# The second layer's modulation: from K-tile matmuls to sums on VectorE

## The chip, the cores and the metric

The kernel runs on one core of one Trainium2 chip. TensorE does matmuls, VectorE and ScalarE elementwise work, GpSimd little here; SyncE (SP) issues nearly all DMAs. All engines run side by side and each works through its own queue in order. The metric is device microseconds of one execution; lower is better.

## The reference, cut to what matters

Two layers over 256 latent tokens and 256 context tokens of width 1024. Each layer begins with a modulation that depends on nothing but the two condition vectors:

```
ada_lat = silu(c) @ w_ada[layer] + b_ada[layer]          # 1024 -> 6144
ada_ctx = silu(c_ctx) @ w_ada[layer] + b_ada[layer]
sh1, sc1, g1, sh2, sc2, g2 = split(ada_lat, 6)           # the same six for ctx
u = modulate(rmsnorm(h, gains[0]), sh1, sc1)             # x * (1 + sc) + sh
h = h + g1 * rmsnorm(mixer(u), gains[1])
h = h + g2 * rmsnorm(mlp(modulate(rmsnorm(h, gains[2]), sh2, sc2)), gains[3])
```

In the second (last) layer the context goes into the mixer only (`need_ctx` is false): of the context's six parts only `sh1` and `sc1` are used there. The MLP is `square(relu(x @ w1)) @ w2`, 1024 to 4096 to 1024.

## The kernel before

Both streams lie side by side as 512 columns of activations. Every big product is computed in split precision: a weight tile of 128x2048 is loaded into one of two `raw` buffers (`ra` in the traces, `RAW=2`), ScalarE rounds each half of it to `wh` (128x1024), VectorE writes the rest `wl = ra - wh`, and TensorE makes three matmuls per K-tile: with `wh` and the rounded activations, `wh` and their rest, `wl` and the rounded ones (`weight`, line 552). `wh` and `wl` have four buffers each (`WB=4`), so a half can be ready while TensorE works on up to three others.

The order of the program is that of a scheduler that models the engines; what is written under a high priority comes first. Background work comes in generators in a queue `bg`: each call of `bg.step()` runs the first generator to its next `yield`. In layer 0, after the output projection, `bg` gets the second layer's modulation in three parts s = 0, 1, 2 of 2048 columns each and the second layer's filters (lines 1492 to 1495). The steps are then taken once for each of the 16 weight tiles of the first MLP product (line 1546) and of those of the second (line 1558, 8 tiles for each half of the output columns), and what is left is drained where layer 1 begins (line 1561).

`ada_steps` (line 366) takes, for each of eight K-tiles, a `raw` buffer, loads 128x2048 of `w_ada` into it and multiplies it with `cst[:, k, :]`: 128 x 32 with silu(c) and silu(c_ctx) in columns 0 and 1 and zeros elsewhere. The four matmuls of a K-tile write four strips of 32 partitions of one PSUM tile and run side by side; a matmul in f32 shows as two instructions in the trace, so a K-tile is a group of eight, `px<-ra,k`. After eight K-tiles the PSUM tile is copied, transposed and put into columns (`ada_cols`, used by `modulation`), and for s > 0 multiplied with gains and written to DRAM as gate rows.

`AM` (line 315) are four 128x512 tiles for the masked scores of the HGRN2 branch. Their upper triangles must be zero, since `copy_predicated` (line 975) writes the others only. They are idle between the branch of layer 0 and that of layer 1.

In the second MLP product `hpart` (line 1498) splits the activations on VectorE as well: a `CAST` to the rounded part and a subtraction for the rest, four K-tiles for each weight tile, shared by the four token tiles.

Of the kernel before, what the change touches and what calls it, by code (L numbers as in the profile page):

```python
# [148 lines left out]
def body(tc, I, out, cfg=None):  # L149
    ctx = ExitStack()  # L150
    with ctx:
        _body(ctx, tc, I, out, cfg or CFG)
# [7 lines left out]
def _body(ctx, tc, I, out, cfg):  # L160
# [12 lines left out]
    def nm(s):  # L173
        counter[0] += 1
        return f"{s}{counter[0]}"

    def blk(dt=F32, p=128, w=512, late=""):

        x = bp.tile([p, w], dt, tag="b", name=nm("b"), padded_shape=[128, 512])
        if late and late in cfg["LATE"]:  # L180
            nc.gpsimd.memset(x[:, 0:1].bitcast(F32) if dt is not F32 else x[:, 0:1], 0.0)
        return x

    def tmp(dt=F32, p=128, w=512, late=""):
        x = tp.tile([p, w], dt, tag="t", name=nm("t"), padded_shape=[128, 512])
        if late and late in cfg["LATE"]:
            nc.gpsimd.memset(x[:, 0:1], 0.0)
        return x
# [4 lines left out]
    def psm():  # L193
        return pm.tile([128, 512], F32, tag="m", name=nm("pm"))

    def psx(kind):
        for i, (kinds, n) in enumerate(cfg["PX"]):
            if kind in kinds:
                return px.tile([128, 512], F32, tag=f"x{i}", name=nm("px"), bufs=n)

    def kt(shape, dt=F32, name="k"):
        return keep.tile(shape, dt, name=nm(name))
# [22 lines left out]
    dve, act, pe, pool = InOrder(nc.vector), InOrder(nc.scalar), InOrder(nc.tensor), nc.gpsimd  # L225
# [20 lines left out]
    def sigmoid():  # L246
        era("sigmoid_and_others")
# [7 lines left out]
    def tt(o, a, b, op):  # L255
        dve.tensor_tensor(o, a, b, op=op)

    def mul(o, a, b):
        tt(o, a, b, ALU.mult)

    def add(o, a, b):
        tt(o, a, b, ALU.add)
# [4 lines left out]
    def stt(o, a, s, b, op0=ALU.mult, op1=ALU.add):  # L267
        dve.scalar_tensor_tensor(o, a, s, b, op0=op0, op1=op1)

    def ts(o, a, s1, s2=None, op0=ALU.mult, op1=ALU.add):  # L270
        if s2 is None:
            dve.tensor_scalar(o, a, s1, None, op0=op0)
        else:
            dve.tensor_scalar(o, a, s1, s2, op0=op0, op1=op1)

    def mm(p, l, r, start, stop, **k):
        return pe.matmul(p, l, r, start=start, stop=stop, **k).ins
# [8 lines left out]
    dma = nc.sync.dma_start  # L286
# [18 lines left out]
    def col(l, name, i, n=1):  # L305
        return vec[l][:, V[name] + i:V[name] + i + n]
# [7 lines left out]
    AM = []  # L314
    for d in range(4):
        a_t = kt([128, 512])
# [3 lines left out]

    cst = kt([128, 8, 32])
    pool.memset(cst, 0.0)
    csg = kt([128, 8, 2])
    sigmoid()
    fn(csg, cc, AF.Sigmoid)
# [4 lines left out]
    def raw_tile():  # L330
        return wp.tile([128, 2048], F32, tag="raw", name=nm("ra"), bufs=cfg["RAW"])
# [34 lines left out]
    def ada_steps(l, s):  # L366
        acc = psx('a')
        for k in range(8):
            raw = raw_tile()
            dma(raw, I["w_ada"][l, k * 128:k * 128 + 128, s * 2048:s * 2048 + 2048])  # L370
            with tc.high_priority(cfg["AP"]):
                for j in range(4):
                    mm(acc[32 * j:32 * j + 32, :], cst[:, k, :], raw[:, j * 512:j * 512 + 512], k == 0, k == 7,
                       tile_position=(0, 32 * j))
            yield
        rows = tmp()
        dve.tensor_copy(rows, acc)
        pt = psx('a')
        for b in range(4):
            pe.transpose(pt[:, b * 128:b * 128 + 128], rows[:, b * 128:b * 128 + 128], ident)  # L380
        cols = kt([128, 2, 2, 8], name="ac")
        pv = pt.rearrange("p (b j r) -> p r j b", b=4, j=4)
        for r in range(2):
            add(cols[:, r].rearrange("p m (j b) -> p (m j) b", b=4), pv[:, r],
                col(l, "ba", 16 * s, 16).rearrange("p (m b) -> p m b", b=4))
        ada_cols[l, s] = cols
        if s > 0:
            w, j0 = s - 1, 2 * (s - 1)
            gr, br = tmp(), tmp()
            dma(gr, I["gate_rows"][l, w, :, 0])  # L390
            dma(br, I["gate_rows"][l, w, :, 1])
            add(rows, rows, br)
            mul(gr, gr, rows)
            st = dr.tile([2, 2, 512], F32, name=nm("gd"))
            for n in range(2):
                dma(st[:, n, :], gr[32 * (j0 + n):32 * (j0 + n) + 2, :])
            G_rows[l, w] = st
        yield

    def modulation(l, which):  # L400
# [320 lines left out]
    def groups(g, sizes):  # L721

        for n in sizes:
            for _ in range(n):
                next(g)
            yield
        for _ in g:
            yield
# [448 lines left out]
    bg = Pump()  # L1177


    def layer(l, S, xs=None, es=None):  # L1180
# [9 lines left out]
        if l == 1:  # L1190
            raw, bd = raw_tile(), [[None, None], [None, None]]
            for d in range(2):
                for g in range(2):
                    r = raw[:, (2 * d + g) * 512:(2 * d + g) * 512 + 512]
# [128 lines left out]
        pv = [psm() for _ in range(4)]  # L1323
        for r in range(2):
            ws = wide(I["w_i"][l, r])
            for t in range(4):
                for kk in range(4):
                    k = 4 * r + kk
# [69 lines left out]
        m = [blk(late='m' if l == 1 else '') for _ in range(8 // per)]  # L1398
        M = None
        gone = False  # L1400
        for bi, b in enumerate(cfg["ORD"][l]):
# [10 lines left out]
            for r in range(2):  # L1412
# [3 lines left out]
                for i in range(4 * r // per, 4 * (r + 1) // per):  # L1416
                    p = psm()
                    for j in range(per):
                        c = i * per + j - 4 * r
# [5 lines left out]
                    x, a, b_ = m[i], m[i], gates[i]  # L1425
                    if bi == 2 and l == 1:
                        x = tmp()
                        a, b_ = (y.rearrange("p (j c r) -> p j c r", j=2, r=ROWS) for y in (a, b_))
# [61 lines left out]


        if full:
            for s in range(3):
                bg.put(ada_steps(1, s))
            bg.put(groups(filters(1), cfg["FG"]))
        hb, cache = [], {}

# [14 lines left out]
        else:  # L1512
            for r in range(2):
                pt = psx('n')
# [9 lines left out]
        for r in range(0 if full else 2, 16):  # L1524
# [12 lines left out]
            for p in ps:  # L1537
                a, x = tmp(), blk() if full else tmp()
# [183 lines left out]
    for _ in f0:  # L1722
        pass
    bg.put(ada_steps(0, 1))
    bg.put(ada_steps(0, 2))
    S1, es = layer(0, S0, xs)
    layer(1, S1, None, es)


# [14 lines left out]
```

## Time and profile before

| | us |
|---|---|
| median of 3 runs | 1521.4 (1518.2 to 1522.33) |
| the profiled execution | 1519.12 |
| its span, first to last instruction | 1517.3 |
| TensorE busy in it | 1487.6 |
| VectorE busy | 953.8 |
| ScalarE busy | 747.6 |

The profile shows one execution. A group of its table is all instructions with the same engine, operation, tiles and shape; `L217` is the helper through which they are recorded, so the tile names tell them apart. `b`, `t` and `pm`/`px` are pools of blocks, temporaries and PSUM tiles, `k` is any tile that is kept (so `cst`, the identity and the score buffers all read `k`), `h` the residual stream. A timeline row has the start, the length from the first start to the last end, and the count of merged instructions; matmuls overlap, so the starts tell more than the lengths.

### The profile page before, as it was taken

To read this page: it belongs to the slowest core of one execution; us is meant where nothing else is said; L and a number is where in the kernel's file an instruction comes from. 1 tells how busy PE (TensorE), PEld (TensorE's weight loads), DVE (VectorE), ACT (ScalarE), POOL (GpSimd) and SP (SyncE) were. 2 spreads that over 40 slices of the span, in tenths; PEclk is the share of its full clock that TensorE was granted. 3 is DMA by queue.
4 is the path that set the end of the run, shared out by engine and by line. 5 is a ranking of instruction groups with operands and counts; after the bars stand their busy time and mean duration, and the time that the engine had idled before them with its cause. 6 is when DMAs were issued, how large, how long until landed. Compare 5 with 4: busy or idle time off the path is not lost.

```text
span 1517.3 us, 21665 instructions
## 1 busy us (share of the span) xinstructions
PE 1487.6 (98%) x8534; PEld 1228.1 (81%) x8534; DVE 953.8 (63%) x1651; ACT 747.6 (49%) x1188; POOL 20.8 (1%) x234
## 2 busy tenths in 40 slices
PE   7999999999999999999999999999999999999998
PEld 4766877788888888777777777798889999899986
DVE  5776396987535277212135657676989986866544
ACT  6476555543232426433331122567887655565433
POOL 0000000000000000000000000000000000000000
PEclk8999999999999999999999999999999999999999
DMA  9644334323222241543554553322233435444553
GB/s 299 238 186 154 122 139 154 125 72 124 84 89 106 88 162 57 222 166 139 195 203 157 181 183 108 115 98 100 108 112 130 163 140 198 178 157 177 209 194 111
DMA packets 47270, 225.38 MB, mean 149 GB/s; under 512 B 4912, under 2 KB 14768, under 8 KB 23488
## 3 DMA queue, kind: packets, MB, share of 16 engines
q1 hardware_dynamic: 45440, 220.85, 41.0%
q10 hardware_dynamic: 1728, 3.15, 0.6%
q8 instruction: 67, 1.10, 0.3%
q14 instruction: 35, 0.29, 0.1%
HBM read 220.80 MB, written 3.18 MB: 148 GB/s over the span
## 4 chain that ended last, share of the span: by engine, by line
PE 82%; DVE 9%; ACT 4%; DMA 3%; issue 1%; SPq 0%; DVEq 0%; ACTq 0%; POOL 0%; POOLq 0%
PE pm L217 71%; PE px L217 10%; DVE b L217 4%; DVE t L217 3%; ACT b L217 2%; DVE wl L217 2%; DMA ra<-in_w_ada_dram 2%; ACT t L217 1%; ACT wh L217 1%; DMA b<-in_w_ada_dram 1%; DMA ra<-in_w_in_dram 1%; DMA h<-in_x_dram 1%; ACT L217 1%; DVE s L217 0%; DVE h L217 0%
## 5 line engine op out<-in xcount | busy, mean ns | idle before, releaser
L217 PE MATMUL pm<-b,wh 128*128 128x512 f32 (+1 forms) x3264 | 823.7, 342 | 1.7 <-DVE b L217 1.7
L217 PEld LDWEIGHTS pm<-b,wh 128*128 128x128 f32 x3264 | 563.9, 190 | 79.9 <-issue 9.3
L217 DVE TENSOR_TENSOR wl<-ra,wh 128x1024 fp32r<-128x1024 f32 x278 | 338.8, 1223 | 380.8 <-ACT wh L217 372.3
L217 PE MATMUL pm<-b,wl 128*128 128x512 f32 (+1 forms) x1632 | 558.0, 342 | 0.9 <-DVE wl L217 0.9
L217 ACT ACTIVATE wh<-ra 128x1024 fp32r<-128x1024 f32 x278 | 293.0, 1059 | 512.3 <-PE pm L217 471.3
L217 PEld LDWEIGHTS pm<-b,wl 128*128 128x128 f32 x1632 | 309.8, 190 | 43.8 <-issue 9.7
L217 PE MATMUL pm<-wh,b 128*128 128x512 f32 x976 | 304.1, 392 | 0.0
L217 PEld LDWEIGHTS pm<-wh,b 128*128 128x128 f32 x976 | 182.2, 188 | 46.8 <-issue 7.4
L217 PE MATMUL pm<-wl,b 128*128 128x512 f32 x488 | 191.2, 392 | 0.0
L217 DVE TENSOR_TENSOR b<-b,b 128x512 fp32r<-128x512 f32 (+2 forms) x179 | 120.8, 682 | 49.4 <-PE pm L217 32.9
L217 PEld LDWEIGHTS pm<-wl,b 128*128 128x128 f32 x488 | 91.6, 188 | 22.4 <-issue 3.6
L217 PE MATMUL pm<-b,b 128*128 128x256 f32 (+1 forms) x456 | 77.5, 324 | 2.3 <-DVE b L217 2.2
L217 ACT ACTIVATE t<-t 128x512 f32<-128x512 f32 (+3 forms) x124 | 61.0, 525 | 32.6 <-DVE t L217 31.7
L217 PEld LDWEIGHTS pm<-b,b 128*128 128x128 f32 x456 | 66.7, 190 | 11.0 <-DVE b L217 3.6
L217 ACT ACTIVATE t<-pm 128x512 f32<-128x512 f32 (+1 forms) x74 | 42.5, 576 | 62.6 <-PE pm L217 60.1
L217 ACT ACTIVATE b<-pm 128x512 f32<-128x512 f32 x88 | 50.8, 584 | 22.9 <-PE pm L217 13.0
L217 PE MATMUL px<-b,b 128*128 128x128 f32 (+1 forms) x280 | 55.5, 344 | 2.1 <-ACT b L217 1.3
L217 ACT ACTIVATE b<-b 128x512 f32<-128x512 f32 (+1 forms) x80 | 48.9, 628 | 10.8 <-DVE b L217 9.6
L217 ACT ACTIVATE b<-b,k 128x512 f32<-128x512 f32 x64 | 45.9, 739 | 8.5 <-DVE b L217 8.3
L217 PEld LDWEIGHTS px<-b,b 128*128 128x128 f32 x280 | 38.7, 190 | 12.6 <-issue 5.6
L217 PE MATMUL px<-ra,k 128*32 128x512 f32 x320 | 42.0, 604 | 2.4 <-DMA ra<-in_w_ada_dram 2.1
L217 DVE TENSOR_TENSOR t<-t,b 128x512 f32<-128x512 f32 (+2 forms) x78 | 42.0, 563 | 0.1
(107 smaller groups left out, 1018.1 us busy)
## 6 DMA issues: line engine op xcount, KB each, us to landing
ra<-in_w_mlp_dram SPq DMA_DIRECT2D x63, 1024.0 KB, 4.8
ra<-in_w_in_dram SPq DMA_DIRECT2D x58, 1024.0 KB, 4.8
ra<-in_w_ada_dram SPq DMA_DIRECT2D x40, 1024.0 KB, 4.9
ra<-in_w_proj_dram SPq DMA_DIRECT2D x12, 1024.0 KB, 4.8
b<-in_w_ada_dram SPq DMA_DIRECT2D x32, 256.0 KB, 6.0
ra<-in_w_out_dram SPq DMA_DIRECT2D x8, 1024.0 KB, 4.8
ra<-in_w_i_dram SPq DMA_DIRECT2D x4, 1024.0 KB, 5.0
b<-gd SPq DMA_DIRECT2D x12, 256.0 KB, 5.5
```

Of the source, the lines that this page charges most:

```text
L217: r = f(*a, **k)
```

## The change

`ada_steps` keeps the first layer's parts. The second layer's come from a new generator, `ada_second`. It loads `w_ada` in pieces of 128x512 into the four score buffers, in 24 steps of four pieces. VectorE multiplies each piece with the condition's value of each partition (a column of `cst`) and adds it to a running sum of 128x512 in a temporary. For s = 0 two sums are kept for each piece (latent and context) and the steps run over eight K-tiles of the first 1024 columns and then of the second; for s = 1 and 2 there is the latent's sum alone. A piece's buffer is loaded for the next step as soon as its sums are issued. When eight K-tiles are added up, four matmuls with `sel` (ones in one column of 32) add the 128 partitions and put the result where the old groups put theirs; for s = 0 that happens twice, once for each half of the columns, into two rows of the same PSUM tile. What follows is `ada_out`, cut out of `ada_steps`, with a second layout for s = 0. At the end GpSimd zeroes the score buffers.

```
@@ -320,6 +320,10 @@
 
     cst = kt([128, 8, 32])
     pool.memset(cst, 0.0)
+    sel = kt([128, 2, 32])
+    pool.memset(sel, 0.0)
+    for r in range(2):
+        pool.memset(sel[:, r, r:r + 1], 1.0)
     csg = kt([128, 8, 2])
     sigmoid()
     fn(csg, cc, AF.Sigmoid)
@@ -373,16 +377,25 @@
                     mm(acc[32 * j:32 * j + 32, :], cst[:, k, :], raw[:, j * 512:j * 512 + 512], k == 0, k == 7,
                        tile_position=(0, 32 * j))
             yield
+        ada_out(l, s, acc, "(j r)")
+        yield
+
+    def ada_out(l, s, acc, order):
+
         rows = tmp()
         dve.tensor_copy(rows, acc)
         pt = psx('a')
         for b in range(4):
             pe.transpose(pt[:, b * 128:b * 128 + 128], rows[:, b * 128:b * 128 + 128], ident)
         cols = kt([128, 2, 2, 8], name="ac")
-        pv = pt.rearrange("p (b j r) -> p r j b", b=4, j=4)
+        if order == "(j r)":
+            pv = pt.rearrange("p (b m n r) -> p r m n b", b=4, m=2, n=2)
+        else:
+            pv = pt.rearrange("p (b n r m) -> p r m n b", b=4, n=2, r=2)[:, :, :2]
         for r in range(2):
-            add(cols[:, r].rearrange("p m (j b) -> p (m j) b", b=4), pv[:, r],
-                col(l, "ba", 16 * s, 16).rearrange("p (m b) -> p m b", b=4))
+            for m in range(2):
+                add(cols[:, r, m].rearrange("p (n b) -> p n b", b=4), pv[:, r, m],
+                    col(l, "ba", 16 * s + 8 * m, 8).rearrange("p (n b) -> p n b", b=4))
         ada_cols[l, s] = cols
         if s > 0:
             w, j0 = s - 1, 2 * (s - 1)
@@ -395,6 +408,58 @@
             for n in range(2):
                 dma(st[:, n, :], gr[32 * (j0 + n):32 * (j0 + n) + 2, :])
             G_rows[l, w] = st
+
+    def ada_second():
+
+
+        plans = [(s, i) for s in range(3) for i in range(8)]
+
+        def pieces(s, i):
+
+            if s > 0:
+                return [(i, s * 2048 + n * 512, n) for n in range(4)]
+            half, kk = divmod(i, 4)
+            return [(2 * kk + a, half * 1024 + n * 512, n) for a in range(2) for n in range(2)]
+
+        def load(q, plan):
+            k, c, _ = pieces(*plan)[q]
+            dma(AM[q], I["w_ada"][1, k * 128:k * 128 + 128, c:c + 512])
+
+        for q in range(4):
+            load(q, plans[0])
+        acc = None
+        for at_, (s, i) in enumerate(plans):
+            yield
+            rs = (0, 1) if s == 0 else (0,)
+            if i == 0 or (s == 0 and i == 4):
+                sums = {}
+            for q, (k, _, n) in enumerate(pieces(s, i)):
+                for r in rs:
+                    c = cst[:, k, r:r + 1]
+                    if (r, n) in sums:
+                        stt(sums[r, n], AM[q], c, sums[r, n])
+                    else:
+                        sums[r, n] = tmp()
+                        ts(sums[r, n], AM[q], c)
+                if at_ + 1 < len(plans):
+                    load(q, plans[at_ + 1])
+            if s == 0 and i in (3, 7):
+                if i == 3:
+                    acc = psx('a')
+                with tc.high_priority(cfg["AP"]):
+                    for g in (3, 0, 1, 2):
+                        mm(acc[32 * g:32 * g + 32, :], sel[:, i // 4, :], sums[g % 2, g // 2], i == 3, i == 7,
+                           tile_position=(0, 32 * g))
+                if i == 7:
+                    ada_out(1, s, acc, "(n r m)")
+            elif i == 7:
+                acc = psx('a')
+                with tc.high_priority(cfg["AP"]):
+                    for g in (3, 0, 1, 2):
+                        mm(acc[32 * g:32 * g + 32, :], sel[:, 0, :], sums[0, g], True, True, tile_position=(0, 32 * g))
+                ada_out(1, s, acc, "(j r)")
+        for a_t in AM:
+            pool.memset(a_t, 0.0)
         yield
 
     def modulation(l, which):
@@ -1490,8 +1555,7 @@
 
 
         if full:
-            for s in range(3):
-                bg.put(ada_steps(1, s))
+            bg.put(ada_second())
             bg.put(groups(filters(1), cfg["FG"]))
         hb, cache = [], {}
```

How this moves the instructions is shown at three places. `wh1012`/`wl1013` and so on are weight halves; numbers differ between the kernels, names of pools don't.

First place, the first of the new groups, in the first MLP product. TensorE before: a group of the fifth to eighth K-tile amid a half's 24 matmuls (`k17` is `cst`, `px980` the accumulator).

```order
L217 MATMUL pm1017_5475<-b833_4546,wh1014_5470 128x512
L217 MATMUL pm1017_5475<-b825_4538,wl1015_5471 128x512
L217 MATMUL pm1017_5475<-b826_4539,wh1014_5470 128x512
L217 MATMUL pm1017_5475<-b834_4547,wh1014_5470 128x512
L217 MATMUL px980_5295<-ra1046_5680,k17_103 32x512 x4
L217 MATMUL pm1017_5475<-b826_4539,wl1015_5471 128x512
L217 MATMUL pm1017_5475<-b827_4540,wh1014_5470 128x512
L217 MATMUL pm1017_5475<-b835_4548,wh1014_5470 128x512
```

After, the first group: `t985` to `t988` are the four sums of the first 1024 columns, `k18` is `sel`. It stands behind 14 of a half's 24 matmuls.

```order
L217 MATMUL pm1016_5501<-b828_4548,wl1013_5494 128x512
L217 MATMUL pm1016_5501<-b829_4549,wh1012_5493 128x512
L217 MATMUL pm1016_5501<-b837_4557,wh1012_5493 128x512
L217 MATMUL px1022_5571<-t988_5322,k18_105 32x512
L217 MATMUL px1022_5571<-t985_5315,k18_105 32x512
L217 MATMUL px1022_5571<-t986_5317,k18_105 32x512
L217 MATMUL px1022_5571<-t987_5320,k18_105 32x512
L217 MATMUL pm1016_5501<-b829_4549,wl1013_5494 128x512
L217 MATMUL pm1016_5501<-b830_4550,wh1012_5493 128x512
```

Four matmuls on a `raw` tile have become four on four sums; this kernel has four such groups, 24 before.

VectorE in front of that group: the last seven sums (`k13` to `k16` are the score buffers, `k17` is `cst`) and two `wl`. Before, only `wl` of one weight tile after another stand here.

```order
L217 TENSOR_TENSOR wl1025_5579<-ra1023_5576,wh1024_5578 128x1024
L217 SCALAR_TENSOR_TENSOR t986_5317<-k13_95,k17_103,t986_5317 128x512
L217 SCALAR_TENSOR_TENSOR t987_5320<-k14_97,k17_103,t987_5320 128x512
L217 SCALAR_TENSOR_TENSOR t988_5322<-k14_97,k17_103,t988_5322 128x512
L217 SCALAR_TENSOR_TENSOR t985_5315<-k15_99,k17_103,t985_5315 128x512
L217 SCALAR_TENSOR_TENSOR t986_5317<-k15_99,k17_103,t986_5317 128x512
L217 SCALAR_TENSOR_TENSOR t987_5320<-k16_101,k17_103,t987_5320 128x512
L217 TENSOR_TENSOR wl1027_5583<-ra1023_5576,wh1026_5582 128x1024
L217 SCALAR_TENSOR_TENSOR t988_5322<-k16_101,k17_103,t988_5322 128x512
L217 TENSOR_TENSOR wl1040_5663<-ra1038_5660,wh1039_5662 128x1024
```

The group waits for the sum `t988`, which stands behind the `wl` of a weight half that is two halves further on than the one in which the group stands.

Second place, VectorE in the second MLP product, from the `wl` of one weight tile to those of the next. Before (`b1237<-b1081` and the row behind it are a split):

```order
L217 TENSOR_TENSOR wl1230_6706<-ra1228_6703,wh1229_6705 128x1024
L217 TENSOR_TENSOR b1234_6714<-b1067_5821,b1233_6713 128x512
L217 TENSOR_TENSOR wl1232_6710<-ra1228_6703,wh1231_6709 128x1024
L217 CAST b1235_6720<-b1069_5825 128x512
L217 TENSOR_TENSOR b1236_6721<-b1069_5825,b1235_6720 128x512
L217 CAST b1237_6727<-b1081_5899 128x512
L217 TENSOR_TENSOR b1238_6728<-b1081_5899,b1237_6727 128x512
L217 CAST b1239_6734<-b1083_5903 128x512
L217 TENSOR_TENSOR b1240_6735<-b1083_5903,b1239_6734 128x512
L217 TENSOR_TENSOR wl1244_6786<-ra1242_6783,wh1243_6785 128x1024
```

After:

```order
L217 TENSOR_TENSOR b1232_6833<-b1068_5881,b1231_6832 128x512
L217 CAST b1233_6839<-b1070_5885 128x512
L217 SCALAR_TENSOR_TENSOR t1196_6646<-k13_95,k17_103,t1196_6646 128x512
L217 TENSOR_TENSOR b1234_6840<-b1070_5885,b1233_6839 128x512
L217 CAST b1235_6846<-b1082_5977 128x512
L217 SCALAR_TENSOR_TENSOR t1197_6649<-k14_97,k17_103,t1197_6649 128x512
L217 SCALAR_TENSOR_TENSOR t1198_6652<-k15_99,k17_103,t1198_6652 128x512
L217 SCALAR_TENSOR_TENSOR t1199_6655<-k16_101,k17_103,t1199_6655 128x512
L217 TENSOR_TENSOR b1236_6847<-b1082_5977,b1235_6846 128x512
L217 CAST b1237_6853<-b1084_5981 128x512
L217 SCALAR_TENSOR_TENSOR t1196_6646<-k13_95,k17_103,t1196_6646 128x512
L217 TENSOR_TENSOR b1238_6854<-b1084_5981,b1237_6853 128x512
```

Sums stand between the two rows of a split; from one weight tile's `wl` to the next there are four splits as before, and six sums.

Third place, SP in the first MLP product. Before, loads of weights and of `w_ada` alternate:

```order
L549 DMA ra1023_5538<-in_w_mlp1_dram 128x2048
L370 DMA ra1034_5606<-in_w_ada_dram 128x2048
L549 DMA ra1035_5612<-in_w_mlp1_dram 128x2048
L370 DMA ra1046_5680<-in_w_ada_dram 128x2048
L549 DMA ra1047_5686<-in_w_mlp1_dram 128x2048
L370 DMA ra1058_5754<-in_w_ada_dram 128x2048
```

After, weight tiles follow the ring of `raw` alone, and the pieces stand between them:

```order
L426 DMA k13_95<-in_w_ada_dram 128x512
L614 DMA ra1038_5660<-in_w_mlp1_dram 128x2048
L426 DMA k14_97<-in_w_ada_dram 128x512
L426 DMA k15_99<-in_w_ada_dram 128x512
L426 DMA k16_101<-in_w_ada_dram 128x512
L426 DMA k13_95<-in_w_ada_dram 128x512
L426 DMA k14_97<-in_w_ada_dram 128x512
L426 DMA k15_99<-in_w_ada_dram 128x512
L614 DMA ra1049_5740<-in_w_mlp1_dram 128x2048
L426 DMA k16_101<-in_w_ada_dram 128x512
```

A piece waits in SP's queue for the sums that read its buffer, and a weight tile for the `wl` that reads its own; each holds back what stands behind it.

## Rows read from the trace of the kernel before

**Rows 1.** The page: busy us of each engine, share, instructions.
```profile
PE 1487.6 (98%) x8534; PEld 1228.1 (81%) x8534; DVE 953.8 (63%) x1651; ACT 747.6 (49%) x1188; POOL 20.8 (1%) x234
```

**Rows 2.** Stretches of 40 us: busy us (instructions), granted clock, DMA share, GB/s.
```profile
core 0: us, PE busy (x) PEld busy (x) DVE busy (x) ACT busy (x) POOL busy (x), PEclk, DMA share, GB/s
680.00:720.00 40.00, 40.00 (x189) 30.41 (x187) 9.50 (x14) 15.29 (x21) 0.00 (x0) 1.00 0.36 131
840.00:880.00 40.00, 39.92 (x185) 30.09 (x184) 24.35 (x39) 7.51 (x8) 0.00 (x0) 1.00 0.51 182
```

**Rows 3.** Waits of TensorE, 560 to 1000 us: total, times, longest.
```profile
PE px L217 <- DMA ra<-in_w_ada_dram: 0.9, 1, 0.9
```

**Rows 4.** Timeline of TensorE around one group: start, length, instructions.
```profile
665.65 0.62 PE L217 MATMUL pm<-b,wh 128*128 128x512 f32 x2
...
666.33 0.61 PE L217 MATMUL pm<-b,wh 128*128 128x512 f32 x2
...
666.87 1.06 PE L217 MATMUL px<-ra,k 128*32 128x512 f32 x8
...
667.87 0.50 PE L217 MATMUL pm<-b,wl 128*128 128x512 f32 x1
...
668.21 0.62 PE L217 MATMUL pm<-b,wh 128*128 128x512 f32 x2
```

**Rows 5.** Timeline of TensorE: starts of six groups of the second layer.
```profile
607.31 1.92 PE L217 MATMUL px<-ra,k 128*32 128x512 f32 x16
...
750.80 1.07 PE L217 MATMUL px<-ra,k 128*32 128x512 f32 x8
...
762.90 1.07 PE L217 MATMUL px<-ra,k 128*32 128x512 f32 x8
...
812.62 1.06 PE L217 MATMUL px<-ra,k 128*32 128x512 f32 x8
...
819.85 1.06 PE L217 MATMUL px<-ra,k 128*32 128x512 f32 x8 [0.91 <-DMA ra<-in_w_ada_dram]
...
884.37 1.06 PE L217 MATMUL px<-ra,k 128*32 128x512 f32 x8
```

**Rows 6.** Groups of instructions: count, busy us, mean ns, idle before and releasers.
```profile
L217 DVE TENSOR_TENSOR wl<-ra,wh 128x1024 fp32r<-128x1024 f32 x278 | 338.8, 1223 | 380.8 <-ACT wh L217 372.3 <-PE pm L217 3.6 <-PE px L217 2.3
...
L217 ACT ACTIVATE wh<-ra 128x1024 fp32r<-128x1024 f32 x278 | 293.0, 1059 | 512.3 <-PE pm L217 471.3 <-DVE b L217 26.8 <-DMA ra<-in_w_in_dram 7.5
...
L217 DVE TENSOR_TENSOR b<-b,b 128x512 fp32r<-128x512 f32 (+2 forms) x179 | 120.8, 682 | 49.4 <-PE pm L217 32.9 <-ACT b L217 12.9 <-DVE b L217 0.5
...
L217 DVE CAST b<-b 128x512 fp32r<-128x512 f32 x89 | 37.5, 421 | 3.8 <-ACT b L217 2.4 <-PE pm L217 1.0
...
L217 DVE SCALAR_TENSOR_TENSOR h<-t,s,h 128x512 f32<-128x512 f32 x24 | 17.0, 748 | 0.4
...
L217 DVE TENSOR_SCALAR t<-h,s,s 128x512 f32<-128x512 f32 x28 | 14.0, 544 | 0.8
```

**Rows 7.** Timeline of VectorE, first and second MLP product: idle before, releaser.
```profile
749.94 1.23 DVE L217 TENSOR_TENSOR wl<-ra,wh 128x1024 fp32r<-128x1024 f32 x1 [4.21 <-ACT wh L217]
...
850.52 0.69 DVE L217 TENSOR_TENSOR b<-b,b 128x512 fp32r<-128x512 f32 x1 [6.44 <-PE pm L217]
```

**Rows 8.** DMA issues: count, KB each, median us from issue to landing.
```profile
ra<-in_w_ada_dram SPq DMA_DIRECT2D x40, 1024.0 KB, 4.9
...
t<-in_gate_rows_dram SPq DMA_DIRECT2D x8, 256.0 KB, 5.3
...
ra<-in_bd_dram SPq DMA_DIRECT2D x4, 256.0 KB, 2.7
...
t<-in_decay_dram SPq DMA_DIRECT2D x2, 256.0 KB, 6.8
```

**Rows 9.** Timeline of SP between two groups: issues of a weight and a `w_ada` tile.
```profile
751.92 0.33 SPq L549 DMA_DIRECT2D ra<-in_w_mlp_dram  x1
757.88 0.33 SPq L370 DMA_DIRECT2D ra<-in_w_ada_dram  x1
```

## The prediction

> **What bounds the kernel now.** I read four views in this order. First the busy line of the page: TensorE is at work 1487.6 of 1517.3 us, VectorE 953.8 [rows 1]. Then the stretches in which the changed work lies: from 680 to 720 us and from 840 to 880 us TensorE is busy for all, or all but 0.1, of the 40 us, at the full granted clock (1.00, the 2.4 GHz level), while VectorE works 9.5 and 24.4 of 40 us [rows 2]. Third, who made TensorE wait between 560 and 1000 us: one row, 0.9 us in all, for a load of `w_ada` [rows 3]. Fourth, TensorE's timeline, because a busy engine need not be a useful one. The reader is to see there that big matmuls follow each other every 0.227 us (three in 0.68 us, 665.65 to 666.33), that a modulation group starts at 666.87 and that the next big matmul starts at 667.87 [rows 4].
>
> The Trainium skill says in "Perfetto Trace Analysis", section "Identifying the Most-Contended Engine", that matmul busy time is a poor measure for TensorE and that LDWEIGHTS busy is a better one. By it the 81% of weight loads [rows 1] leave room, groups could sit in bubbles, and the change would be worth nothing; that is the third rival below. The trace speaks against it by starts instead of busy time, in the next paragraph.
>
> **What is removed.** The second layer's modulation runs as 24 groups of eight TensorE instructions (four matmuls in two passes), the first two at 607.31, the last at 884.37. Two neighbours are 12.10 us apart (750.80 to 762.90) with 48 big matmuls between [rows 5]. These take 48 x 0.227 = 10.88 us. So a group costs 1.22 us of TensorE's time, its 1.06 us plus refilling the array, and it fills no bubble. 24 x 1.22 = 29.3 us. The one wait for a load, 0.9 us [rows 3, 5], goes as well: 30.2 us. The `wh` and `wl` of the weights stay.
>
> **What is added on TensorE.** Four groups of the same eight instructions (two for s = 0, one each for s = 1 and 2), with a sum in place of the raw tile. Their form is that of the removed ones, so 4 x 1.22 = 4.9 us. Transposes and the copies behind them stay in number. If nothing else happened the balance would be -25.3 us.
>
> **What is added on VectorE.** 64 multiplications and sums for s = 0 (32 pieces, two rows each), 32 each for s = 1 and 2: 128 instructions, of which 16 begin a sum (`tensor_scalar`) and 112 add to one. The nearest rows are of the same shape and memory: `h<-t,s,h` 17.0 us for 24, so 0.71 us of the engine each (0.75 from start to end), and `t<-h,s,s` 14.0 for 28, 0.50 us [rows 6]. 16 x 0.50 + 112 x 0.71 = 88 us. It lies beside TensorE's work, in idle time of 30 of 40 us in the first MLP product and 16 of 40 in the second [rows 2]. The cover is real as long as VectorE's own products for TensorE come in time, and the engine works in order, so I follow what is queued behind a sum.
>
> In the first MLP product these are the weight halves `wl`. They run up to three halves (16 us) ahead of TensorE: VectorE waits for `wh`, and that for TensorE to release a buffer [rows 6, 7]. Six or seven sums between two `wl` make 1.22 + 6.5 x 0.71 = 5.8 us for a half on which TensorE works 24 x 0.227 = 5.44 us. That is 0.4 us of backlog for each of about four halves, and the 16 us swallow it: nothing.
>
> In the second MLP product VectorE also splits four tiles of activations for each weight tile. From the release of a weight buffer it needs 1.06 (`wh`) + 2 x 1.22 (`wl`) + 4 x (0.42 + 0.675) for the splits [rows 6] + 6 x 0.71 for the sums queued among them = 12.1 us. TensorE wants the last split after its 48 matmuls and nine more, 57 x 0.227 = 12.9 us. Before, without the sums and with a group in the step, VectorE had 6.44 us to spare here [rows 7]; now 0.8 us. I take 2 us for five such steps; the bounds are 0 and 8 (a load late by some 1.6 us in each).
>
> **The new waits.** TensorE now waits for a sum where it waited for a load, and the four groups stand in its queue close behind the moment at which the sum can be ready. Group 1 stands 14 matmuls (3.2 us) behind the end of the half that frees a weight buffer, and its last sum is queued behind that buffer's `wl`: 1.06 + 1.22 + 0.75 = 3.0 us, and hand-overs. A hand-over is short: a group begun at 750.80 ends at 751.87 and the load that waits for it is issued at 751.92 [rows 5, 9]; I allow 0.2 us for three. With some backlog, 0.5 us of waiting. Group 2: 26 matmuls, 5.9 us, against 1.06 + 1.22 + 5 x 0.71 + 0.2 = 6.0: 0.5 with backlog. Group 3: 23 matmuls, 5.2 us, against 1.06 + 1.22 + 4 x 0.71 + 0.2 = 5.3: 0.4 with a late load. Group 4: 44 matmuls, 10.0 us, against 1.06 + 2.44 + 5 x 0.42 + 4 x 0.675 + 5 x 0.71 + 0.2 = 12.0: 1.8 to 2.0, I take 1.8. Together 3.2 us. Behind a waiting group stand all big matmuls, so each of these microseconds is lost in full; behind a waiting sum stand `wl` and the splits, priced above.
>
> **The loads.** The same bytes of `w_ada` come as 96 pieces of 256 KB instead of 24 of 1 MB. No row shows such a piece into a score buffer. The nearest: the four `bd` pieces of 256 KB land 2.7 us after issue, a gate row piece 5.3, a decay piece 6.8 [rows 8]. With 2.7 a score buffer goes round in 0.75 + 0.05 + 0.33 (issue, [rows 9]) + 2.7 = 3.8 us. For s = 1 the order leaves 5.4 us for a K-tile (its eight K-tiles stand beside eight halves of 5.44 us), for s = 2 about 7.6 (5.75 sums to a step of 10.9 us, four sums to a K-tile), for s = 0 about 6.9 (eight sums and one `wl`). I take the `bd` row, the one of the same kind (several pieces back to back, from an otherwise quiet queue), so nothing is late; the 5.3 and 6.8 rows carry two rivals. Weight loads get the whole two-tile ring again: a `w_ada` tile was issued at 757.88, a ring's turn behind a weight tile at 751.92 [rows 9]. That helps them start earlier and frees no time on TensorE, which did not wait for them.
>
> The Trainium skill says in "DMA: Bandwidth & Descriptors", section "Queues, rings and completion order", that the loads of one issuing engine share its rings and are taken in order. By it a piece issued right behind a 1 MB weight tile cannot land before it. The row that bears on it agrees: a 1 MB tile lands after 4.9 us, and the gate row issued behind one after 5.3 [rows 8]. If that held for every second K-tile, half of the next case's delay would come, and the sum would be -16, or 1506 us.
>
> **Other parts.** The two memsets of `sel` and four of the score buffers lie on GpSimd, which is 1% busy [rows 1]. The first four pieces are loaded during layer 0. The filters of the second layer now come earlier, under TensorE's full stretch instead of at the layers' junction; TensorE waits at neither [rows 3]. I count all three as nothing, with 2 us to either side for layer 0's shifted order.
>
> **Sum.** -30.2 + 4.9 + 3.2 + 2.0 = -20.1 us. Against the profiled execution (1519.1 us; its span is 1517.3) that is 1499.0. The median of the runs is 1521.4, 2.3 above it, so 1501.3 on that footing: I say 1501.
>
> **Rivals.** *Late pieces, still faster.* If the pieces land like the gate row (5.3 us), a buffer's turn is 6.4 us, 1.0 more than the order leaves for s = 1: seven refills make 7 us at group 3. For s = 0, where two sums use a piece, the turn is 7.2 against 6.9: 2 us over both halves. 9 us of waiting more: -11, 1510 us. For it: pieces stand behind weight tiles in the one queue. Against: only 22 of the 96 stand directly behind one.
> *Slower: the score buffers' turn becomes the bound.* One set of four buffers, reloaded only after use. With 6.8 us a turn is 7.9 us for s = 1 (2.5 over, seven times: 17.4), 8.7 for s = 0 (1.8 over, three times in each half: 10.8) and 0.3 over for s = 2 (2.3): 30.5 us of waiting. -25.3 + 30.5 + 3 = +8, 1529 us. It decides from a landing of about 6.4 us on, where the delays reach the 22 us that are to be lost. Against: the DMA engines are half busy here (shares of 0.36 and 0.51, [rows 2]).
> *No change.* The groups fill bubbles of TensorE, or something else sets its pace of 12.10 us: about 1521. The count of starts speaks against it.
>
> **Chances.** Forecast 0.75, its own range 1494 to 1506; late pieces 0.15; no change 0.05; slower 0.05. The range goes from 1493 (no wait at all, 1496, less the 3 us by which runs differ) to 1512 (late pieces, and 2 for layer 0). A measurement of this kernel tells 0.3%, some 4.6 us, from no change. Faster by more: 0.75 + 0.15 = 0.90; within: 0.05; slower: 0.05.
>
> **What would show it.** Right: big matmuls of the MLP products 48 to 10.9 us without a gap, four `px<-t,k` groups of about 1.06 us with waits for VectorE of 0 to 2 us before each, VectorE's busy time up by some 88 us, the score buffers' pieces landing in about 3 us. Wrong: TensorE waiting for VectorE (`b` or `wl`) at every step of the second MLP product, VectorE waiting for `w_ada` pieces in rows of their own, sums that take well over 0.75 us, or an idle TensorE in a stretch that the change doesn't touch.

## The result, and the profile after

The changed kernel takes 1504.4 us (median of 4 runs, 1500.4 to 1504.6) against 1521.9 us (4 runs, 1518.2 to 1523.4) for the kernel before: ratio 0.9889, 95% interval 0.9873 to 0.9906. That is 17.5 us less, where 20.1 were forecast. The profiled execution (1504.6 us, span 1502.8) is one of the longer ones and stands 14.5 us below that of before.

So the first question is where in the span the time went. A good clock for that is an instruction that both kernels run in the same order: ScalarE's `wh`, the first half of a weight's split, 278 of them. Two rows of its timeline mark the changed stretch, the last `wh` before the first removed group and the first one behind the layers' junction (columns: start, length, instruction). Before:

```profile
571.24 1.05 ACT L217 ACTIVATE wh<-ra 128x1024 fp32r<-128x1024 f32 x1
...
1002.82 2.07 ACT L217 ACTIVATE wh<-ra 128x1024 fp32r<-128x1024 f32 x2
```

After:

```profile
572.48 1.05 ACT L217 ACTIVATE wh<-ra 128x1024 fp32r<-128x1024 f32 x1
...
986.95 2.06 ACT L217 ACTIVATE wh<-ra 128x1024 fp32r<-128x1024 f32 x2
```

The stretch took 431.6 us and takes 414.5: 17.1 less, nearly the 17.5 of the medians. Ahead of it the changed kernel lost 1.2 us in layer 0, behind it 1.4 in layer 1. This profile and the nine of the experiments below have between -3.1 and +1.4 us against before ahead of the stretch, and between -0.1 and +2.4 behind it, so I compare by the stretch. For the 1.4 us behind it the rows show a cause that is not the change. In layer 1 TensorE waits 2.51 us for VectorE in both kernels, and in this profile it is granted about half of its clock afterwards, in the one of before all of it (TensorE's timeline, and the stretch of 2 us behind the wait with the columns of [rows 2]; the changed kernel, then the one before):

```profile
1113.53 1.26 PE L217 MATMUL px<-t 128*128 128x128 f32 x20 [2.51 <-DVE t L217]
1114.00:1116.00 2.00, 2.00 (x24) 1.71 (x24) 1.72 (x5) 0.65 (x2) 0.43 (x11) 0.52 0.00 0
...
1129.38 1.04 PE L217 MATMUL px<-t 128*128 128x128 f32 x20 [2.51 <-DVE t L217]
1130.00:1132.00 2.00, 2.00 (x30) 1.83 (x30) 1.95 (x5) 1.20 (x4) 0.43 (x11) 1.00 0.00 0
```

All eleven profiles of this document have this wait (2.50 or 2.51 us), and seven of them the lower clock behind it.

The rows that answer to those of before. The page's busy line (busy us, share, instructions), to [rows 1]:

```profile
PE 1466.1 (98%) x8374; PEld 1227.7 (82%) x8374; DVE 1033.4 (69%) x1789; ACT 747.2 (50%) x1188; POOL 23.0 (2%) x241
```

TensorE has 21.5 us less work, VectorE 79.6 more. Stretches of 40 us in the first and second MLP product, to [rows 2]; the last row is that of the kernel before for the second:

```profile
680.00:720.00 40.00, 39.71 (x181) 31.86 (x180) 23.29 (x39) 15.25 (x21) 0.00 (x0) 1.00 0.54 194
...
800.00:840.00 40.00, 40.00 (x179) 33.10 (x178) 37.63 (x60) 8.51 (x8) 0.00 (x0) 1.00 0.69 230
...
800.00:840.00 40.00, 39.09 (x187) 28.67 (x186) 21.75 (x37) 7.42 (x7) 0.00 (x0) 1.00 0.44 160
```

TensorE is as full as it was, and VectorE, which had 30 and 18 of 40 us free, now has 17 and 2. Who made TensorE wait from 560 to 1000 us (total, times, longest), to [rows 3]; then TensorE's timeline at the four new groups and at the junction, to [rows 5]:

```profile
PE px L217 <- DVE t L217: 6.1, 4, 3.9
```

```profile
645.35 1.06 PE L217 MATMUL px<-t,k 128*32 128x512 f32 x8 [0.24 <-DVE t L217]
...
693.17 1.07 PE L217 MATMUL px<-t,k 128*32 128x512 f32 x8 [0.29 <-DVE t L217]
...
748.06 0.61 PE L217 MATMUL pm<-b,wh 128*128 128x512 f32 x2
752.57 1.93 PE L217 MATMUL px<-t,k 128*32 128x512 f32 x8 [3.90 <-DVE t L217]
754.43 0.80 PE L217 MATMUL pm<-b,wl 128*128 128x512 f32 x1
755.02 0.93 PE L217 MATMUL pm<-b,wh 128*128 128x512 f32 x2
755.80 0.40 PE L217 MATMUL pm<-b,wl 128*128 128x512 f32 x1
...
847.57 1.06 PE L217 MATMUL px<-t,k 128*32 128x512 f32 x8
...
966.60 1.86 PE L217 MATMUL px<-k,t 128*128 128x128 f32 x15 [1.66 <-DVE t L217]
```

Groups 1 and 2 wait 0.24 and 0.29 us, group 3 waits 3.90, group 4 not at all; the fourth of the four waits, 1.66 us, belongs to transposes at the junction, which waited for nothing before [rows 3]. Behind the wait of group 3 the work is slow for a while: the group takes 1.93 us in place of 1.06, and the next three matmuls take 1.37 us (754.43 to 755.80) in place of 0.80 behind an old group (667.87 to 668.67 in the timeline of before). The granted clock says why (stretches of 2 us; the columns are those of [rows 2]):

```profile
750.00:752.00 2.00, 0.00 (x0) 0.00 (x0) 1.43 (x3) 0.00 (x0) 0.00 (x0) 1.00 0.76 253
752.00:754.00 2.00, 1.43 (x8) 0.20 (x8) 0.51 (x1) 0.00 (x0) 0.00 (x0) 0.57 0.95 321
754.00:756.00 2.00, 2.00 (x8) 1.32 (x5) 0.67 (x1) 0.70 (x2) 0.00 (x0) 0.58 0.97 364
756.00:758.00 2.00, 2.00 (x10) 1.61 (x9) 0.56 (x1) 0.53 (x1) 0.00 (x0) 1.00 0.48 185
```

After idling for 3.9 us TensorE was granted 0.57 and 0.58, close to its lower level (1.2 GHz), until about 756 us. By starts, the two matmuls ahead of the group, the group and the three behind it took 7.74 us (748.06 to 755.80), and 2.34 around an old group (666.33 to 668.67). Group 3 thus cost 5.4 us above its own work, 3.9 of waiting and 1.5 of clock that no wait shows.

Why its sum was late stands in VectorE's timeline (idle time before and its releaser in brackets), and in the landing of the pieces (count, KB each, median us from issue to landing), from 640 to 700 us, most of it s = 0, and from 720 to 755 us, the end of s = 1 and the first pieces of s = 2:

```profile
730.60 2.87 DVE L217 SCALAR_TENSOR_TENSOR t<-k,k,t 128x512 f32<-128x512 f32 x4 [1.33 <-DMA k<-in_w_ada_dram]
734.02 0.75 DVE L217 SCALAR_TENSOR_TENSOR t<-k,k,t 128x512 f32<-128x512 f32 x1 [0.56 <-DMA k<-in_w_ada_dram]
...
739.03 0.75 DVE L217 SCALAR_TENSOR_TENSOR t<-k,k,t 128x512 f32<-128x512 f32 x1 [1.14 <-DMA k<-in_w_ada_dram]
739.70 1.22 DVE L217 TENSOR_TENSOR wl<-ra,wh 128x1024 fp32r<-128x1024 f32 x1
743.50 0.75 DVE L217 SCALAR_TENSOR_TENSOR t<-k,k,t 128x512 f32<-128x512 f32 x1 [2.58 <-DMA k<-in_w_ada_dram]
...
751.76 0.75 DVE L217 SCALAR_TENSOR_TENSOR t<-k,k,t 128x512 f32<-128x512 f32 x1 [0.29 <-DVE t L217]
```

```profile
k<-in_w_ada_dram SPq DMA_DIRECT2D x19, 256.0 KB, 2.9
```

```profile
k<-in_w_ada_dram SPq DMA_DIRECT2D x27, 256.0 KB, 5.1
ra<-in_w_mlp_dram SPq DMA_DIRECT2D x3, 1024.0 KB, 6.9
```

In the first stretch a piece lands after 2.9 us, in the second after 5.1. The counts are those of the issues; the trace has a landing for 8 of the 19 and 11 of the 27, and for one of the three weight tiles. SP issues a weight tile and then up to nine pieces behind it, and the landing goes by how close behind: of the 92 pieces loaded from 560 to 860 us the trace has 33 landings, 14 of pieces issued within 4 us behind a weight tile (3.6 to 6.9 us, median 4.9) and 19 of others (2.6 to 4.0, median 2.8). SP's timeline has the weight tile at 735.94 and the first pieces at 736.60, and the chain of waits has the piece whose sum is the one at 744.62 (start, length):

```profile
737.98 6.55 DMA k<-in_w_ada_dram
```

The last sum ends at 752.5, where TensorE has been standing since 748.7.

### The profile page after: what moved, and what is told of

Its sections match the earlier page's. It is cut to its first block, busy times and chain, and to the rows that moved or that the text cites. A ratio compares the mean times of both kernels' runs of the same rounds, so it can differ in the third digit from the quotient of the medians.

```text
span 1502.8 us, 21672 instructions
## 1 busy us (share of the span) xinstructions
PE 1466.1 (98%) x8374; PEld 1227.7 (82%) x8374; DVE 1033.4 (69%) x1789; ACT 747.2 (50%) x1188; POOL 23.0 (2%) x241
## 4 chain that ended last, share of the span: by engine, by line
PE 46%; DVE 6%; ACT 3%; DMA 2%; issue 1%; DVEq 0%; ACTq 0%; SPq 0%
PE pm L217 42%; PE px L217 4%; DVE t L217 2%; DMA k<-in_w_ada_dram 2%; DVE b L217 2%; ACT b L217 1%; DVE wl L217 1%; ACT t L217 1%; ACT wh L217 1%; ACT L217 0%; DVE s L217 0%; DVE h L217 0%; ACT s L217 0%; DVE k L217 0%; DVEq L1804 0%
## 5 line engine op out<-in xcount | busy, mean ns | idle before, releaser
L217 DVE TENSOR_TENSOR b<-b,b 128x512 fp32r<-128x512 f32 (+2 forms) x179 | 120.4, 680 | 21.5 <-ACT b L217 12.9
L217 DVE SCALAR_TENSOR_TENSOR t<-k,k,t 128x512 f32<-128x512 f32 x112 | 78.8, 746 | 13.9 <-DMA k<-in_w_ada_dram 13.5
L217 ACT ACTIVATE t<-px 128x384 f32<-128x384 f32 (+3 forms) x50 | 22.0, 440 | 41.8 <-PE px L217 41.3
```

The costliest lines, as they stand in the source:

```text
L217: r = f(*a, **k)
```

## The experiments

All are compared with the kernel before on the same chip, and with the changed kernel by the stretch between the two `wh` (414.5 us; 416.4 in a second profile, below). These two are 2.0 us apart, so a smaller difference counts only where a row shows where it arises.

**Group 3 later.** Only the group of s = 1 moves, 25 matmuls down TensorE's order; all other instructions stay where they are.

```diff
-                with tc.high_priority(cfg["AP"]):
+                with tc.high_priority(cfg["AP"] if s == 2 else 200):
```

> The changed kernel with one edit: the modulation group for s = 1 has a lower priority and stands 25 big matmuls (25 x 0.227 = 5.7 us) later in TensorE's order; nothing else moves. Theory: the group's wait of 3.90 us for its sum, and about 1.5 us of half clock behind it, are pure loss. So TensorE's wait there falls to 0 to 0.3 us, the granted clock from 720 to 760 us stays 1.00, the half around it takes 5.44 + 1.22 = 6.7 us in place of 12.1, and the time falls by about 5.4 us, to 1499. Rival (VectorE is behind as a whole, the wait only changes its place): a new wait for wl or for the sum of 3 us or more a few matmuls later, and 0 to -1.5 us.

Measured: 1496.6 us, ratio 0.9848 (0.9825 to 0.9871); the stretch takes 409.4 us, 5.0 less. TensorE at the group, and VectorE's waits for pieces from 720 to 760 us, which were 7.7 us in 8 times:

```profile
754.22 1.07 PE L217 MATMUL px<-t,k 128*32 128x512 f32 x8
```

```profile
DVE t L217 <- DMA k<-in_w_ada_dram: 9.0, 9, 3.4
```

The pieces are as late as before, the group does not wait, the granted clock from 720 to 760 us is 1.00, and no new wait takes its place. Wait and clock were pure loss.

**Filters later.** Two empty steps put the filters back where they stood.

```diff
         for a_t in AM:
             pool.memset(a_t, 0.0)
         yield
+        yield
+        yield
```

> The changed kernel with one edit: two empty steps behind the second layer's sums, so that the filters of the second layer start in the step in which they started before the change. Theory: the wait of 1.66 us of TensorE for VectorE's t at the layers' junction (between 960 and 1000 us) came because some 7 us of filter matmuls that stood there before now run earlier; put back, they cover the chain again: the wait goes, -1.7 us. Rival (the chain of the norm is late for another reason, as the sums): the wait stays, 0 us.

Measured: 1502.1 us, ratio 0.9885 (0.9865 to 0.9906); the stretch takes 414.1 us. As a whole this is no difference. Its parts are these: the 16 transposes at the junction run without a wait,

```profile
961.80 1.91 PE L217 MATMUL px<-k,t 128*128 128x128 f32 x16
```

and from the first `wh` behind the last of the old groups to the one behind the junction it takes 115.08 us (867.15 to 982.23), as before (887.74 to 1002.82), where the changed kernel takes 116.95 (870.00 to 986.95) and so loses 1.9. Against that, group 3 waited 4.51 us here and was on the lower clock for longer, 1.2 us more in all than in the changed kernel, and group 2 waited 0.96 in place of 0.29.

**Both** of these edits.

> Both edits: the group for s = 1 25 matmuls later and the filters two steps later. Theory: the two gains add, -5.4 - 1.7 = -7 us against the changed kernel, about 1497. Rival: each stays as if alone or nothing, 1502 to 1504.

Measured: 1495.7 us, ratio 0.9840 (0.9820 to 0.9859); stretch 408.8 us, 5.7 less than the changed kernel's. Group 3 and the junction wait for nothing; groups 1 and 2 waited 0.72 and 1.33 us in this execution, which is the rest of the 7. The time is 0.9 us below that of the first experiment, less than either's runs differ, so what the filters' edit is worth in whole time is not shown.

**18 of the 24 groups left out**, in the kernel before.

```diff
             with tc.high_priority(cfg["AP"]):
-                for j in range(4):
+                for j in range(4) if l == 0 or k in (0, 7) else ():
```

> The kernel before with one edit: of the 24 modulation groups of the second layer only six run (first and last K-tile of each s), the other 18 are left out; their loads of 1 MB stay, but nothing reads them. Theory (a group costs its 1.06 us and the refilling of the array, 1.22 us): 18 x 1.22 = 22 us less, and up to 0.9 for the wait for a load, so 1522 - 22 to 23 = about 1499. Rival (groups fill bubbles of TensorE, or something else sets its pace of 12.10 us for two halves): 0 to -3 us.

Measured: 1495.4 us, ratio 0.9839 (0.9820 to 0.9858). The stretch goes from 431.6 to 408.7 us (`wh` at 568.27 and 976.95): 22.9 less, of which 0.9 was the wait for a load:

```profile
568.27 1.05 ACT L217 ACTIVATE wh<-ra 128x1024 fp32r<-128x1024 f32 x1
...
976.95 2.05 ACT L217 ACTIVATE wh<-ra 128x1024 fp32r<-128x1024 f32 x2
```

22.0 / 18 = 1.22 us for a group, the price read from starts, not from busy time (the medians, 24.2 us apart, would make it 1.3). Groups fill no bubbles.

**A second set of buffers for s = 1.** Every other K-tile's pieces go into four tiles of the pool `bp`, from which its sums then read; the group stands five matmuls earlier than in the changed kernel.

```diff
-            dma(AM[q], I["w_ada"][1, k * 128:k * 128 + 128, c:c + 512])
+            dma(buf(q, plan), I["w_ada"][1, k * 128:k * 128 + 128, c:c + 512])
...
+        def buf(q, plan):
+            s, i = plan
+            if s == 1 and i % 2 and not second:
+                second.extend(blk() for _ in range(4))
+            return second[q] if s == 1 and i % 2 else AM[q]
```

> The changed kernel with one edit: for s = 1 every other K-tile's four pieces go into a second set of four buffers, so a piece is issued a K-tile (four sums and more) earlier. Theory (group 3 waited 3.9 us because a buffer's turn, with pieces that land 5 us after issue behind a weight tile, was longer than the 5.44 us of a half): VectorE's waits for pieces from 720 to 760 us fall from 7.7 us to under 1.5, group 3, which stands five matmuls (1.1 us) earlier here, waits 0 to 1.5 us and the clock stays 1.00: 4 to 5.5 us faster than the changed kernel, ratio to before 0.985 to 0.986. Rival (VectorE does not keep up by its own work): it waits for no piece, the group still waits 3 us or more, ratio 0.989.

Measured: 1497.3 us, ratio 0.9862 (0.9845 to 0.9878); the stretch takes 408.7 us, 5.7 less. TensorE at group 3, and VectorE's waits from 720 to 760 us:

```profile
744.41 1.06 PE L217 MATMUL px<-t,k 128*32 128x512 f32 x8
```

```profile
DVE wl L217 <- ACT wh L217: 14.2, 5, 4.2
DVE t L217 <- DMA b<-in_w_ada_dram: 3.6, 2, 2.3
DVE t L217 <- DMA k<-in_w_ada_dram: 0.4, 1, 0.4
```

VectorE still waits 4.0 us for pieces, more than the 1.5 expected, but it is ahead again (it waits 14.2 us for `wh`), and the group finds its sum ready, though five matmuls earlier. So the buffers' turn was the cause and not VectorE's own work.

**Pieces from another queue.** GpSimd issues the 32 pieces of s = 1; the group stands where it stood in the first experiment.

```diff
-            dma(AM[q], I["w_ada"][1, k * 128:k * 128 + 128, c:c + 512])
+            (pool.dma_start if plan[0] == 1 else dma)(AM[q], I["w_ada"][1, k * 128:k * 128 + 128, c:c + 512])
```

> The kernel with group 3 later (first experiment), and its 32 pieces for s = 1 issued by GpSimd instead of SP, so that they stand behind no weight tile in a queue. Theory A (order within SP's queue makes pieces late): the pieces land in about 3 us, VectorE's waits for pieces from 720 to 760 us fall from 9.0 us in the first experiment to under 2. Theory B (a weight tile under way takes the DMA engines, whichever queue a piece stands in): pieces still take about 5 us beside a weight tile, the waits stay 5 us or more. The time is that of the first experiment, 1496 to 1497, by both, since its group no longer waits.

Measured: 1498.1 us, ratio 0.9860 (0.9846 to 0.9875), stretch 409.9 us; 0.5 us slower in the stretch than the first experiment, and the group waited 0.69 us. VectorE's waits for pieces from 720 to 760 us:

```profile
DVE t L217 <- DMA k<-in_w_ada_dram: 11.2, 9, 3.8
```

They grew from 9.0 to 11.2 us: standing behind no weight tile in a queue did not help, and Theory A, by which they fall under 2, falls. Theory B shows in the landings. SP issues weight tiles at 726.86 and 741.70; GpSimd's four pieces behind the first of them, and its six pieces ahead of the second (least, median, most, us from issue to landing):

```profile
DMA to landing us min/median/max: 5.3/5.9/5.9
...
DMA to landing us min/median/max: 3.0/3.2/4.0
```

Of all 32 pieces, 15 were issued within 4 us behind a weight tile and took 3.8 to 5.9 us (median 5.2), the other 17 took 2.9 to 4.0 (median 3.2). So a weight tile under way makes a piece late from another queue too. Why the waits grew by 2.2 us is not shown: an issue takes GpSimd 0.54 us, against 0.33 on SP, and starts 0.3 us behind the sum that frees the buffer (725.69 to 725.99), where SP's starts at once (731.36 to 731.38). The Trainium skill says in "DMA: Bandwidth & Descriptors", section "Queues, rings and completion order", that a DMA engine goes round between the queues that have work for it. By that a piece shares the engines with a weight tile under way from whatever queue it comes, and this run agrees with it, with 5.2 us beside a weight tile against 3.2.

**The sums of s = 2 twice.**

```diff
                         stt(sums[r, n], AM[q], c, sums[r, n])
+                        if s == 2:
+                            stt(sums[r, n], AM[q], c, sums[r, n])
```

> The changed kernel with the sums for s = 2 that add to one done twice: 28 instructions more on VectorE in the second MLP product, 28 x 0.66 = 18 us, 3.4 for each step of 10.9 us; group 4 stands later accordingly. Theory (VectorE, busy 37.6 of 40 us from 800 to 840, has about 0.65 us to spare in a step, and its splits stand behind the sums): TensorE waits for b or wl in each of some five steps, 2 to 3 us each, 12 to 15 us slower than the changed kernel, ratio to before 0.997 to 0.999. Rival (the 6.44 us that it had to spare in a step before are mostly there still): under 3 us slower, ratio below 0.991.

Measured: 1503.9 us, ratio 0.9899 (0.9884 to 0.9914); stretch 415.4 us, 0.9 more than the changed kernel. My theory of the step falls, though the rival's reason was not right either. Two stretches of 40 us in the second MLP product:

```profile
800.00:840.00 40.00, 40.00 (x177) 32.87 (x176) 40.00 (x63) 8.52 (x8) 0.00 (x0) 1.00 0.55 173
840.00:880.00 40.00, 39.87 (x178) 31.30 (x176) 39.75 (x68) 9.97 (x15) 2.32 (x4) 1.00 0.54 190
```

VectorE has nothing to spare, 40.00 and 39.75 of 40 us, and TensorE still works 40.00 and 39.87. The order spreads the doubled sums over more steps: group 4 stands 141 matmuls later and starts at 878.96 in place of 847.57. In VectorE's timeline from 815 to 845 us at most four sums follow one another before the next row of a split or the next `wl`; that this is why they came in time is my reading, which no run tests alone.

**The changed kernel again (no edit), and the second set of buffers with the filters later (the two edits above).**

> The changed kernel itself, to compare it on one chip with the next. Theory: group 3 waits for its sum 3.5 to 4.5 us in every execution (3.9, 4.5 and 4.1 in three profiles so far), the junction another 1.7; ratio to before 0.988 to 0.990. If the wait were an accident of one execution it would be gone here and the ratio 0.985.

> The second set of buffers for s = 1 and the filters two steps later, together. Theory: group 3 waits 0 to 0.5 us, nothing waits at the junction, so 5.5 + 1.8 = 7.3 us less than the changed kernel on the same chip, about 1496, ratio to before 0.984. Rival: the 1.8 us of the junction come back behind it, 1497 to 1498, ratio 0.986.

Measured: the changed kernel 1503.1 us, ratio 0.9899 (0.9880 to 0.9917); group 3 waits 4.03 us, stretch 416.4. The wait recurs in every profile in which the order and the buffers are those of the change: 3.90, 4.51, 4.06 and 4.03 us. The version with two sets and later filters: 1495.4 us, ratio 0.9845 (0.9828 to 0.9862), 7.7 us below the changed kernel on the same chip, stretch 408.0 us. From 560 to 1000 us one wait is left, of 1.45 us, at group 2. The rival's ratio, 0.986, lies at the edge of the interval, and this profile lost 2.4 us behind the stretch, with the lower clock at two places there; so the stretch shows the junction's gain and the time does not. This version and the one with both orders changed (1495.7) beat both kernels and can't be told from each other.

## Why the prediction was right, and where its terms were not

The direction and the mechanism came out: each group that goes gives back its pitch, and VectorE takes the work in beside TensorE's. The size came out too, forecast -20.1 us, measured -17.5, within the forecast's own range, but in part by luck: two terms were too small by 6.9 us and three too large by 4.3, and they nearly cancel. One of the forecast's own signs of being wrong appeared, VectorE's waits for pieces, 13.5 us of them in all (row below).

| term | forecast | measured |
|---|---|---|
| 24 groups and the wait for a load go | -30.2 | -30.2 (1.22 us each by leaving out 18; the wait is gone) |
| four groups come | +4.9 | +4.9 (at the same price; 1.06 or 1.07 us of work each but for group 3) |
| waits at groups 1 and 2 | +1.0 | +0.5 |
| wait at group 3, and the clock behind it | +0.4 | +5.4 |
| wait at group 4 | +1.8 | 0 |
| splits of the second MLP product late | +2.0 | 0 |
| filters earlier, at the junction | 0 | +1.9 (1.66 of it the wait) |
| sum | -20.1 | -17.5; the stretch shows -17.1 |

*What was removed* held, since it was counted in starts; with profiles of one kernel up to 2.0 us apart, 18 groups tell the price to some 0.1 us. The Trainium skill's rule on LDWEIGHTS busy time ("Perfetto Trace Analysis", section "Identifying the Most-Contended Engine") would have left room for the groups. Here PEld was busy 1228.1 us before [rows 1] and 1227.7 after, while 21.5 us of matmul work went, and the time followed the starts.

*What was added on VectorE* was priced at 88 us and took 85.9:

```profile
L217 DVE SCALAR_TENSOR_TENSOR t<-k,k,t 128x512 f32<-128x512 f32 x112 | 78.8, 746 | 13.9 <-DMA k<-in_w_ada_dram 13.5 <-DVE t L217 0.3
...
L217 DVE TENSOR_SCALAR t<-k,k 128x512 f32<-128x512 f32 x16 | 7.1, 480 | 0.0
```

That it would be hidden was right. My slack of 0.8 us for a step of the second MLP product was wrong in its method: I added durations as if each instruction waited for the one ahead, and put `wh` in series. Back to back they overlap. The step after:

```profile
804.99 2.35 DVE L217 TENSOR_TENSOR wl<-ra,wh 128x1024 fp32r<-128x1024 f32 x2
807.26 0.42 DVE L217 CAST b<-b 128x512 fp32r<-128x512 f32 x1
807.60 0.75 DVE L217 SCALAR_TENSOR_TENSOR t<-k,k,t 128x512 f32<-128x512 f32 x1
808.26 0.69 DVE L217 TENSOR_TENSOR b<-b,b 128x512 fp32r<-128x512 f32 x1
808.87 0.42 DVE L217 CAST b<-b 128x512 fp32r<-128x512 f32 x1
...
815.87 2.35 DVE L217 TENSOR_TENSOR wl<-ra,wh 128x1024 fp32r<-128x1024 f32 x2
```

A sum advances the engine by 0.66 us (807.60 to 808.26), a cast by 0.34, a subtraction by 0.61, two `wl` by 2.27; the step closes in 10.88 us (804.99 to 815.87), just TensorE's 48 x 0.227. The same error made group 4 late by 1.8 us on paper; its sum was in fact ready in time.

*The loads* were the step that failed. I took one landing, 2.7 us, for all 96 pieces, from `bd` pieces of "an otherwise quiet queue", and that row is one landing: the trace has it for one of the four pieces. Away from weight tiles the 2.7 was right (median 2.8). But SP's queue is not quiet: within 4 us behind a tile the pieces took 4.9 (median). I had written down a case of -16 us for it, and kept it beside the sum because only some pieces stand directly behind a tile (17 of them in SP's timeline, not 22). What counted is that one late round in each two K-tiles is enough: two rounds of sums took 11.7 and 12.9 us (718.90, 730.60, 743.50 in VectorE's timeline), two halves take TensorE 10.88. So the term that failed is the wait at group 3, 0.4 us in the sum and 5.4 measured. The rival "late pieces" had the place, group 3, and asked 7 us of waiting; 3.9 us of waiting and 1.5 of clock came. Its second place, s = 0, did not show.

*The junction* was counted as nothing because TensorE waited at neither place before. That was the wrong reading: it did not wait because the filters' matmuls stood there. Taken away, the chain through VectorE behind them showed; put back in the second experiment, they covered it again.

## What to carry to other kernels

Price work on a full engine by the starts of its neighbours (with the group and without), and work on a half-full engine by its pitch back to back, not by mean durations. A load's landing time belongs to a place in the program: read it from a row in which the same large loads are under way, look how many landings the row stands on, and ask how many late rounds a ring of buffers can take before its consumer stands. Work that waits for something slow should not have the highest priority: 25 matmuls further down the order, the same late sum cost nothing. And where no wait shows at a place from which work is moved away, that work may be the cover.

## What the runs showed of the hardware that I had not expected

A single wait of 3.9 to 4.5 us in a full stretch cost another 1.5 to 2.7 us (four profiles), because TensorE was granted about half of its clock afterwards (0.57 in the profile shown); with the wait gone the clock stayed at 1.00. Waits of up to 1.7 us at the same groups and at the junction left no such trace, and one wait of 2.51 us in layer 1, the same in all profiles, left it in seven of eleven. The profiles without a lowered clock behind the stretch are within 0.1 us of each other there, those with one are 0.9 to 1.7 us longer: whole times of one kernel differ by that. In the changed kernel a load of 256 KB landed after 2.8 us (median of 19), and after 4.9 (median of 14) when it was issued within 4 us behind one of 1 MB; issued by GpSimd in place of SP (sixth experiment) it was 3.2 and 5.2. And VectorE at 40.00 and 39.75 of 40 us left TensorE at work for 40.00 and 39.87.
